# A sliding-window copy with DMA queues alone: twelve staged batches for eleven, half-window copies throughout, and the spilled halves last

## The chip, the cores and the metric

The kernel runs on one core of a Trainium2 chip. A core has engines that compute (TensorE, VectorE, ScalarE, GpSimd), SyncE, and 16 DMA engines that copy. Any of SyncE, ScalarE and GpSimd can issue a copy; each of the three has its own DMA queue, and all three queues are served by the same 16 DMA engines. The metric is the time of one execution on the device in microseconds (us).

## The reference

The input is 32 batches of 4096 rows of 256 floats. A window is 64 rows, and windows start every 32 rows, so each batch has 127 windows and every row but the first and the last 32 of a batch appears in two of them.

```
batch, length, dim = (32, 4096, 256)          # float32; window_size 64, stride 32
n_windows = (length - window_size) // stride + 1      # 127
result = np.zeros((batch, n_windows, window_size, dim), dtype=np.float32)
for i in range(n_windows):
    start = i * stride
    result[:, i] = x[:, start:start + window_size].copy()
```

Nothing is computed: 134 MB are read, and 266.3 MB are written. The unit of all that follows is a block of 32 rows, 32 KB. A batch is 128 blocks; window w of a batch is the blocks w and w + 1, its two halves.

## The kernel before, in words

Batches are copied in two ways.

A **direct** batch goes from DRAM to DRAM. `windows` (line 29) copies n consecutive windows, whole (64 KB each) or only half 0 or half 1 of each (32 KB each). Its argument `piece` is the largest run of one packet in bytes, 32 KB unless given. With 16 windows in a copy, each of the 16 DMA engines gets one window. `columns` (line 40) copies a few windows cut into 16 strips of 4 KB, so that each engine gets a strip of each window.

A **staged** batch goes through on-chip memory. `Staging` (line 70) has six buffers of 128 partitions x 32 KB. `load` puts block p of the batch into partition p (4 MB); `store` writes all 128 partitions out twice, once as half 0 and once as half 1 of the windows, in packets of 16 KB. A block is so read once and written twice. As there are 127 windows and 128 blocks, each of the two stores spills one half window over into the neighbouring batch: half 0 of block 127 lands in the first window of the next batch, and half 1 of block 0 in the last window of the batch before. So those two windows of the neighbours must be written after the stores have landed.

Three engines issue:

- ScalarE (`ring_s`, queue q10) runs `Staging.run`: in groups of six, first the loads of the group, then its stores. Staged are batches 1, 4, 7, ..., 31, eleven of them (the last with its blocks shifted by one, so that it takes along the last block of batch 30). A load waits for the stores that used its buffer before, a store waits for its load.
- SyncE (`ring_d`, queue q1) issues the direct batches in pieces of 16 windows, 147 of them (lines 175 to 190). A counter `share` chooses for each piece whether it goes out as one copy of whole windows or as two copies of halves: more halves while ScalarE's queue is expected to hold loads, fewer while it holds stores.
- GpSimd (`ring_r`, queue q0) starts when the last piece but one has landed (semaphore `near`, line 192) and copies the `edges` (15 windows of each direct batch beside a staged one, which include the windows that were spilled over), each after a wait for the stores of the staged neighbour. A copy of columns follows.

SyncE then waits for the stores of the last staged batch (line 202), copies two last windows as columns, and waits for all semaphores. A queue's packets are taken in order; between the queues an engine takes turns packet by packet. A copy ends on each engine with a completion packet of 4 bytes, which takes a turn as well.

The changed parts are `Staging.load` and `Staging.store` and everything from line 143 to the end of the kernel function.

Of the kernel before, what the change touches and what calls it, by code (L numbers as in the profile page):

```python
# [8 lines left out]
DIRECT, IN, OUT = 32768, 16384, 16384  # L9


class Copier:
# [36 lines left out]
    def load(self, q, t, b, c, rows):  # L49

        p, step, n, unit = rows
        return q.dma_start(
            out=t[p : p + (n - 1) * step + 1 : step, :],
            in_=self.xap(b * self.nb + c + p // unit, [[step // unit * self.blk, n], [1, self.blk]]),
            max_dma_last_dim=IN,
        )

    def store(self, q, t, b, c, rows, half):


        p, step, n, unit = rows
        w = b * self.nw + c + p // unit - half
        return q.dma_start(
            out=self.oap(2 * w + half, [[2 * step // unit * self.blk, n], [1, self.blk]]),
            in_=t[p : p + (n - 1) * step + 1 : step, :],
            max_dma_last_dim=OUT,
        )


class Staging:  # L70
# [14 lines left out]

    def load(self, q, g):
        i = g % len(self.tiles)
        b, c, n = self.items[g]
        if self.count[self.stored[i]]:
            q.wait_ge(self.stored[i], self.count[self.stored[i]])  # L90
        step = 128 // n
        parts = [(k, 4, 32, 1) for k in range(4)] if g == 0 else [(0, step, n, step)]
        for rows in parts:
            self.issue(self.c.load(q, self.tiles[i], b, c, rows), self.loaded[i])
        self.after_load[g] = self.count[self.loaded[i]]

    def store(self, q, g):
        i = g % len(self.tiles)
        b, c, n = self.items[g]
        q.wait_ge(self.loaded[i], self.after_load[g])  # L100
        step = 128 // n
        parts, end = [((0, step, n, step), 0), ((0, step, n, step), 1)], []
        if g == len(self.items) - 1:

            parts = [((0, 1, 128, 1), 1), ((0, 1, 32, 1), 0)]
            end = [(96, 1, 32, 1)] + [(32 + k, 4, 16, 1) for k in range(4)]
        for rows, half in parts:
            self.issue(self.c.store(q, self.tiles[i], b, c, rows, half), self.stored[i])
        for rows in end:
            self.issue(self.c.store(q, self.tiles[i], b, c, rows, 0), self.ended)  # L110
        self.after_store[g] = self.count[self.stored[i]]

    def wait_stored(self, q, g):
# [12 lines left out]
@with_exitstack  # L126
def kernel(
    ctx: ExitStack,
    tc: tile.TileContext,
    x: bass.AP,  # L130
    window_size: bass.AP,
    stride: bass.AP,
    out: bass.AP,
):
    nc = tc.nc
    W, S = int(window_size), int(stride)
    B, L, D = x.shape
    n_win = (L - W) // S + 1
    assert out.shape == (B, n_win, W, D)
    c = Copier(x, out, B, L, D, W, S, n_win)  # L140


    staged = [*range(1, B, 3)]
    items = [(b, -1 if b == B - 1 else 0, c.nb) for b in staged]
    place = {b: g for g, (b, _, n) in enumerate(items) if n == c.nb}
    direct = [b for b in range(B) if b not in staged]
    pool = ctx.enter_context(tc.tile_pool(name="xb", bufs=1))
    st = Staging(c, tc, pool, x.dtype, items, 6)
    ring_d, ring_s, ring_r = nc.sync, nc.scalar, nc.gpsimd
    done = tc.alloc_semaphore("done")  # L150
    near = tc.alloc_semaphore("near")
    rest = tc.alloc_semaphore("rest")
    total = {done: 0, near: 0, rest: 0}

    def count(dma, sem):
        dma.then_inc(sem, 16)
        total[sem] += 16

    sixteens = []
    for b in direct:
        w = 15 if b - 1 in staged else 0
        sixteens += [(b, w + 16 * j) for j in range((c.nw - w) // 16)]
    singles = [(B - 1, c.nw - 1, 1)]
    edges = [(b, 0 if b - 1 in staged else 112, 15) for b in direct[:-1]]
    last = B - 2
    edges.append((last, 112, 4))

    first_loads, loads, stores = 6 * 17, 5 * 17, 6 * 34  # L170
    turns = share = 0
    with tc.tile_critical():  # L172
        st.run(ring_s)

        for i, (b, w) in enumerate(sixteens):
            sem = near if i == len(sixteens) - 2 else done
            second = turns - first_loads - stores
            loading = turns < first_loads or 0 <= second < loads
            share += 120 if turns < 16 or -8 <= second < 16 else 90 if loading else 18
            if share >= 120:  # L180
                share -= 120
                turns += 4
                count(c.windows(ring_d, b, w, 16, 0), done)
                count(c.windows(ring_d, b, w, 16, 1), sem)
            else:
                turns += 3
                count(c.windows(ring_d, b, w, 16), sem)
            if i == len(sixteens) // 2:
                for b, w, half in singles:
                    count(c.windows(ring_d, b, w, 1, half, 2048), done)  # L190

        ring_r.wait_ge(near, 16)
        for b, w, n in edges:
            for k in (b - 1, b + 1):
                if k in place and b != last:
                    st.wait_stored(ring_r, place[k])
            count(c.windows(ring_r, b, w, n), rest)


        count(c.columns(ring_r, last, 116, 9), rest)  # L200
        ring_r.drain()  # L201
        st.wait_stored(ring_d, place[B - 1])
        count(c.columns(ring_d, last, 125, 2), done)
        total[st.ended] = st.count[st.ended]
        for sem, n in total.items():
            ring_d.wait_ge(sem, n)
# [35 lines left out]
```

## Time and profile before

| | |
|---|---|
| time, median of 3 runs | 753.98 us (753.93 to 756.95) |
| span of the profiled execution | 742.1 us |
| time around the span, by the median | 11.9 us |
| copied by the DMA engines | 313.26 MB, mean 422 GB/s |
| memory read, written | 220.95 MB, 267.09 MB |
| copies issued by SyncE | 92 of 1024 KB, 110 of 512 KB, 2 small |
| copies issued by ScalarE | 14 loads, 27 stores |
| copies issued by GpSimd | 22 |
| first GpSimd copy issued | 649.1 us |
| SyncE's last copy issued | 723.8 us |

The time of a run is a little longer than the span of the profiled execution, which goes from the first to the last instruction. The page's DMA line shows in 40 equal slices how busy the 16 DMA engines were, in tenths. The table of queues gives for each queue its packets, its MB, and the time that its packets took as a share of the 16 engines' time over the span; so the shares add up to the whole when the engines are full. The same view can be asked for any stretch of the span. The trace also holds a record of every single packet with its start, its duration, its queue and its size.

### The profile page before, as it was taken

Reading aid. Unit: us, or ns where it says so; the run is one execution under the profiler, and the core shown is the slowest. Engines: PE = TensorE matmul, PEld = TensorE weight load, DVE = VectorE, ACT = ScalarE, POOL = GpSimd, SP = SyncE. Lnnn points to the kernel's source line nnn. Section 1 sums busy time; section 2 is a strip of 40 time slices with the busy share of each in tenths; the row PEclk is TensorE's granted clock in tenths of the full one; section 3 lists DMA queues with packets and bytes.
Section 4 is the critical chain, followed back from the end, with each engine's and each line's share of the span. In section 5 each row is a group of like instructions: output and inputs, shape, how many; then the busy total and the mean of one; then the engine's idle time right before and its main releaser. Section 6 shows DMA issues by size and latency. Waiting matters only on the chain.

```text
span 742.1 us, 323 instructions
## 1 busy us (share of the span) xinstructions
POOL 12.7 (2%) x26
## 2 busy tenths in 40 slices
POOL 0000000000000000000000000000000000050100
DMA  8999999999999999999999999999999999999996
GB/s 361 424 430 427 435 431 428 423 435 425 428 427 426 428 428 420 429 435 427 427 427 412 433 435 431 427 436 432 434 424 429 430 424 426 428 435 432 421 420 253
DMA packets 18290, 313.26 MB, mean 422 GB/s; under 512 B 4336, under 2 KB 4336, under 8 KB 4528
## 3 DMA queue, kind: packets, MB, share of 16 engines
q1 hardware_dynamic: 8016, 154.32, 48.8%
q10 hardware_dynamic: 9104, 138.41, 44.0%
q0 software_dynamic: 1168, 20.51, 6.6%
q14 instruction: 2, 0.02, 0.0%
HBM read 220.95 MB, written 267.09 MB: 658 GB/s over the span
## 4 chain that ended last, share of the span: by engine, by line
another core or an unknown queue 92%; POOL 2%; issue 0%; POOLq 0%; SPq 0%
POOL out_dram L34 2%; POOLq L201 0%; POOLq L237 0%; SPq L172 0%; POOLq L114 0%
## 5 line engine op out<-in xcount | busy, mean ns | idle before, releaser
L34 POOL DMA_DIRECT2D out_dram<-in_x_dram x21 | 12.0, 575 | 685.4 <-DMA out_dram<-in_x_dram 648.7
L44 POOL DMA_DIRECT2D out_dram<-in_x_dram x1 | 0.6, 581 | 0.0
L223 POOL MEMSET const-float32-0.0<- 128x1 f32 x1 | 0.1, 98 | 0.2 <-issue 0.2
L223 POOL MEMSET const-bfloat16-1.0<- 128x1 bf16 x1 | 0.1, 101 | 0.0
L223 POOL MEMSET const-float32-1.0<- 128x1 f32 x1 | 0.1, 98 | 0.0
L223 POOL MEMSET const-uint8-127<- 128x1 uint8 x1 | 0.1, 98 | 0.0
## 6 DMA issues: line engine op xcount, KB each, us to landing
out_dram<-in_x_dram SPq DMA_DIRECT2D x92, 1024.0 KB, 99.8
out_dram<-xb ACTq DMA_DIRECT2D x21, 4096.0 KB, 138.5
out_dram<-in_x_dram SPq DMA_DIRECT2D x110, 512.0 KB, 90.2
xb<-in_x_dram ACTq DMA_DIRECT2D x10, 4096.0 KB, 130.5
out_dram<-in_x_dram POOLq DMA_DIRECT2D x20, 960.0 KB, 37.9
xb<-in_x_dram ACTq DMA_DIRECT2D x4, 1024.0 KB, 15.7
out_dram<-xb ACTq DMA_DIRECT2D x2, 1024.0 KB, 110.5
out_dram<-xb ACTq DMA_DIRECT2D x4, 512.0 KB, 94.4
```

What stands on the lines that cost most here:

```text
L34: return q.dma_start(out=self.oap((b * self.nw + w0) * 2 + h, [[2 * blk, n], row]), in_=self.xap(b * self.nb + w0 + h, [[blk, n], row]), m ...
L44: return q.dma_start(out=self.oap((b * self.nw + w0) * 2, [[part, 16], [2 * self.blk, n], row]), in_=self.xap(b * self.nb + w0, [[part, 16 ...
L223: nc = _bacc.Bacc("TRN2", target_bir_lowering=False, num_devices=1)
```

## The change

Staged are now twelve batches: 1, 4, 7, 10, 13, 16, 18, 20, 22, 25, 28 and 30. `store` splits some of its two stores into two copies of 64 partitions (even and odd ones), in an alternating pattern, and the last batch's into four.

SyncE's direct copies, 280 now, are all of halves of 16 windows. The counter `share` is gone. Twenty halves at the end of the list are held back, and two more, `spoilt` (which contain the half windows that the stores of batch 30 spill over), are put last of all. SyncE issues 258 halves and a copy of columns, waits for the semaphore `back`, issues the twenty, waits for the first two stores of batch 30, and issues the two.

GpSimd starts when the fourth half from the end of the 258 has landed. Its list of 22 edges is preceded by three whole windows and eight windows in halves; the edges beside batch 28 are moved to the end of the list. Every third edge goes in 16 KB pieces. The semaphore `back` is raised by the 18th of the 22 edges.

```diff
     def store(self, q, g):
         i = g % len(self.tiles)
-        b, c, n = self.items[g]
+        b = self.items[g]
         q.wait_ge(self.loaded[i], self.after_load[g])
-        step = 128 // n
-        parts, end = [((0, step, n, step), 0), ((0, step, n, step), 1)], []
         if g == len(self.items) - 1:
-
-            parts = [((0, 1, 128, 1), 1), ((0, 1, 32, 1), 0)]
-            end = [(96, 1, 32, 1)] + [(32 + k, 4, 16, 1) for k in range(4)]
...
+            parts = [(0, 2, 1), (1, 2, 0), (0, 2, 0), (1, 2, 1)]
+        else:
+            parts = [(k, n, half) for half in (0, 1) for n in (2 if (2 * g + half) % 4 < 2 else 1,) for k in range(n)]
+        for m, (k, n, half) in enumerate(parts):
+            sem = self.ended if g == len(self.items) - 1 and m > 1 else self.stored[i]
+            self.issue(self.c.store(q, self.tiles[i], b, 0, (k, n, 128 // n, 1), half), sem)
...
-    staged = [*range(1, B, 3)]
-    items = [(b, -1 if b == B - 1 else 0, c.nb) for b in staged]
+    staged = [1, 4, 7, 10, 13, 16, 18, 20, 22, 25, 28, B - 2]
...
-    sixteens = []
+    sixteens, edges = [], []
+    last, held = B - 1, 20
     for b in direct:
-        w = 15 if b - 1 in staged else 0
-        sixteens += [(b, w + 16 * j) for j in range((c.nw - w) // 16)]
-    singles = [(B - 1, c.nw - 1, 1)]
-    edges = [(b, 0 if b - 1 in staged else 112, 15) for b in direct[:-1]]
-    last = B - 2
-    edges.append((last, 112, 4))
-
-    first_loads, loads, stores = 6 * 17, 5 * 17, 6 * 34
-    turns = share = 0
+        first = 0 if b == last or b - 1 not in staged else 7 if b + 1 in staged[:-1] else 15
+        sixteens += [(b, first + 16 * j) for j in range(7)]
+        if b != last:
+            edges += [(b, w, n) for w, n in ((0, first), (first + 112, 15 - first)) if n]
+    odd = -sum(n for _, _, n in edges) % 16
+    late = [e for e in edges if staged[-2] in (e[0] - 1, e[0] + 1)]
+    edges = [e for e in edges if e not in late] + late
+    halves = [(b, w, half) for b, w in sixteens for half in (0, 1)]
+    spoilt = [(last - 2, c.nw - 16, 1), (last, 0, 0)]
+    halves = [h for h in halves if h not in spoilt]
+    middle, main = len(halves) // 2, len(halves) - held
+
+    def blocks(part, sem=done):
+        for b, w, half in part:
+            count(c.windows(ring_d, b, w, 16, half), sem)
+
     with tc.tile_critical():
         st.run(ring_s)

-        for i, (b, w) in enumerate(sixteens):
-            sem = near if i == len(sixteens) - 2 else done
...
-            share += 120 if turns < 16 or -8 <= second < 16 else 90 if loading else 18
-            if share >= 120:
-                share -= 120
-                turns += 4
-                count(c.windows(ring_d, b, w, 16, 0), done)
-                count(c.windows(ring_d, b, w, 16, 1), sem)
-            else:
-                turns += 3
-                count(c.windows(ring_d, b, w, 16), sem)
...
+        blocks(halves[:middle])
+        count(c.columns(ring_d, last, 120 + odd, 7 - odd), done)
+        blocks(halves[middle : main - 4])
+        blocks(halves[main - 4 : main - 3], near)
+        blocks(halves[main - 3 : main])

         ring_r.wait_ge(near, 16)
+        count(c.windows(ring_r, last, 112, odd), rest)
+        for half in (0, 1):
+            count(c.windows(ring_r, last, 112 + odd, 8, half, DIRECT // 2), rest)
+        for i, (b, w, n) in enumerate(edges):
             for k in (b - 1, b + 1):
-                if k in place and b != last:
+                if k in staged[:-1]:
                     st.wait_stored(ring_r, place[k])
-            count(c.windows(ring_r, b, w, n), rest)
-
-
-        count(c.columns(ring_r, last, 116, 9), rest)
+            count(c.windows(ring_r, b, w, n, piece=DIRECT if i % 3 != 0 else DIRECT // 2), back if i == len(edges) - len(late) - 3 else rest)
         ring_r.drain()
-        st.wait_stored(ring_d, place[B - 1])
-        count(c.columns(ring_d, last, 125, 2), done)
+
+        ring_d.wait_ge(back, 16)
+        blocks(halves[main:])
+        st.wait_stored(ring_d, place[B - 2])
+        blocks(spoilt)
```

More of the change, by code (lines that the diff above doesn't have):

```diff
@@ L87, in load @@
         i = g % len(self.tiles)
-        b, c, n = self.items[g]
+        b = self.items[g]
         if self.count[self.stored[i]]:
             q.wait_ge(self.stored[i], self.count[self.stored[i]])
-        step = 128 // n
-        parts = [(k, 4, 32, 1) for k in range(4)] if g == 0 else [(0, step, n, step)]
+        parts = [(k, 4, 32, 1) for k in range(4)] if g == 0 else [(0, 1, 128, 1)]
         for rows in parts:
-            self.issue(self.c.load(q, self.tiles[i], b, c, rows), self.loaded[i])
+            self.issue(self.c.load(q, self.tiles[i], b, 0, rows), self.loaded[i])
         self.after_load[g] = self.count[self.loaded[i]]
@@ L98, in store @@
         i = g % len(self.tiles)
-        b, c, n = self.items[g]
+        b = self.items[g]
         q.wait_ge(self.loaded[i], self.after_load[g])
-        step = 128 // n
-        parts, end = [((0, step, n, step), 0), ((0, step, n, step), 1)], []
         if g == len(self.items) - 1:
-            parts = [((0, 1, 128, 1), 1), ((0, 1, 32, 1), 0)]
-            end = [(96, 1, 32, 1)] + [(32 + k, 4, 16, 1) for k in range(4)]
[L107 to L110, printed above, removed]
+            parts = [(0, 2, 1), (1, 2, 0), (0, 2, 0), (1, 2, 1)]
[4 more added lines that the diff above has]
+            self.issue(self.c.store(q, self.tiles[i], b, 0, (k, n, 128 // n, 1), half), sem)
         self.after_store[g] = self.count[self.stored[i]]
@@ L140 @@
     c = Copier(x, out, B, L, D, W, S, n_win)
-    staged = [*range(1, B, 3)]
-    items = [(b, -1 if b == B - 1 else 0, c.nb) for b in staged]
-    place = {b: g for g, (b, _, n) in enumerate(items) if n == c.nb}
+    staged = [1, 4, 7, 10, 13, 16, 18, 20, 22, 25, 28, B - 2]
+    place = {b: g for g, b in enumerate(staged)}
     direct = [b for b in range(B) if b not in staged]
     pool = ctx.enter_context(tc.tile_pool(name="xb", bufs=1))
-    st = Staging(c, tc, pool, x.dtype, items, 6)
+    st = Staging(c, tc, pool, x.dtype, staged, 6)
     ring_d, ring_s, ring_r = nc.sync, nc.scalar, nc.gpsimd
@@ L152 @@
     rest = tc.alloc_semaphore("rest")
-    total = {done: 0, near: 0, rest: 0}
+    back = tc.alloc_semaphore("back")
+    total = {done: 0, near: 0, rest: 0, back: 0}
     def count(dma, sem):
@@ L172 @@
     with tc.tile_critical():
         st.run(ring_s)
-        for i, (b, w) in enumerate(sixteens):
-            sem = near if i == len(sixteens) - 2 else done
-            second = turns - first_loads - stores
-            loading = turns < first_loads or 0 <= second < loads
-            share += 120 if turns < 16 or -8 <= second < 16 else 90 if loading else 18
-            if share >= 120:
-                share -= 120
-                turns += 4
-                count(c.windows(ring_d, b, w, 16, 0), done)
-                count(c.windows(ring_d, b, w, 16, 1), sem)
-            else:
-                turns += 3
-                count(c.windows(ring_d, b, w, 16), sem)
-            if i == len(sixteens) // 2:
-                for b, w, half in singles:
-                    count(c.windows(ring_d, b, w, 1, half, 2048), done)
+        blocks(halves[:middle])
@@ L192 @@
+        count(c.columns(ring_d, last, 120 + odd, 7 - odd), done)
+        blocks(halves[middle : main - 4])
+        blocks(halves[main - 4 : main - 3], near)
+        blocks(halves[main - 3 : main])
         ring_r.wait_ge(near, 16)
-        for b, w, n in edges:
+        count(c.windows(ring_r, last, 112, odd), rest)
+        for half in (0, 1):
+            count(c.windows(ring_r, last, 112 + odd, 8, half, DIRECT // 2), rest)
+        for i, (b, w, n) in enumerate(edges):
             for k in (b - 1, b + 1):
-                if k in place and b != last:
+                if k in staged[:-1]:
```

## The prediction, made before the changed kernel ran

> **What bounds the kernel now.** Nothing is computed; the 16 DMA engines copy, fed by three queues: q1 (SyncE, direct copies), q10 (ScalarE, staged batches), q0 (GpSimd, edges). I read the page's DMA line and queue table first, then the DMA view of three stretches, then the DMA queue's waits.
>
> ```profile
> DMA  8999999999999999999999999999999999999996
> DMA packets 18290, 313.26 MB, mean 422 GB/s; under 512 B 4336, under 2 KB 4336, under 8 KB 4528
> ## 3 DMA queue, kind: packets, MB, share of 16 engines
> q1 hardware_dynamic: 8016, 154.32, 48.8%
> q10 hardware_dynamic: 9104, 138.41, 44.0%
> q0 software_dynamic: 1168, 20.51, 6.6%
> ...
> HBM read 220.95 MB, written 267.09 MB: 658 GB/s over the span
> ```
>
> The engines are full from the first slice to the last: the three shares sum to 99.4% of 742.1 us, 737.7 us of packet time on each engine. They move 313.26 MB: a direct byte passes once (266.3 MB are the output), a staged byte twice, once as load and once as store. The single packets of the trace run from 2.4 to 739.7 us. What remains to be asked is whether an engine is slowed by memory or is at its own pace. The stretch 430 to 520 us:
>
> ```profile
> DMA packets 2321, 38.82 MB, mean 431 GB/s; under 512 B 589, under 2 KB 589, under 8 KB 589
> ## 3 DMA queue, kind: packets, MB, share of 16 engines
> q1 hardware_dynamic: 1162, 20.88, 54.0%
> q10 hardware_dynamic: 1159, 17.94, 46.5%
> ```
>
> 46.5% of 16 x 90 us is 669.6 us for 17.94 MB, 37.3 us per MB, or 0.611 us for a staged packet of 16,384 B. q1's is 37.2 us per MB, its completion packets included. The trace's packet records say the same: 98% of the 16 KB packets here take 0.611 us and 97% of the 32 KB packets 1.213 us, with 0.009 us for a completion packet. And 150 to 390 us:
>
> ```profile
> DMA packets 5700, 102.67 MB, mean 428 GB/s; under 512 B 1216, under 2 KB 1216, under 8 KB 1232
> ## 3 DMA queue, kind: packets, MB, share of 16 engines
> q1 hardware_dynamic: 2852, 58.89, 57.7%
> q10 hardware_dynamic: 2848, 43.78, 42.9%
> ```
>
> The same sums give 37.6 us per MB on both queues, 1% more: some packets are stalled (31% of the 32 KB ones). q1 has more of the engines here, because its whole-window copies give two 32 KB packets to one completion packet, and the queues take turns packet by packet. Last, 736 to 740 us, where one engine still works and the others are done:
>
> ```profile
> DMA packets 25, 0.11 MB, mean 29 GB/s; under 512 B 6, under 2 KB 6, under 8 KB 22
> ```
>
> Memory is nearly idle here, and the 16 KB packets still take 0.611 us. So 0.611 and 1.213 us are the engine's own pace, and nothing that spares memory makes a packet shorter. Over the run, 313.26 MB x 37.3 / 16 = 730 us; the 737.7 us measured are about 8 us of stalls above it. That is all that a gentler pattern can give back, besides an end in which 15 engines finish between 734 and 737 us and one at 739.7 (one was already 3 us behind the others at 652 us, where q1's main stream ends).
>
> ```profile
> SPq L44 <- DMA out_dram<-xb: 169.3, 1, 169.3
> SPq L206 <- DMA out_dram<-in_x_dram: 15.8, 1, 15.8
> ```
>
> SyncE idles 169.3 us before its last copy and nothing suffers, since the other queues keep the engines full.
>
> **The change, part by part**, in packet time per engine.
>
> *A twelfth staged batch.* Its load is 4 MB: 16 packets of 16 KB on each engine. Its stores are 32 more. 11 x 48 = 528 packets become 576: +48 x 0.611 = +29.3 us.
>
> *SyncE's copies.* 110 half-window copies and 92 whole-window ones are 294 packets of 32 KB; 280 halves (258, 20 held back, 2 spilled) are 280: -14 x 1.213 = -17.0 us. The two spilled halves are written twice: each staged batch stores 128 rows twice where its output has 127 windows, and that is inside the counts of both versions.
>
> *GpSimd's copies.* Before: 304 whole windows, 38 packets of 32 KB an engine, and a columns copy of nine 4 KB packets at 0.159 us. After: 3 + 8 + 285 = 296 windows, 37 packets: -1.2 - 1.4 us. SyncE's columns copy grows from two to four such packets: +0.3 us. Eight of the edges and the two half copies go in 16 KB or half-window pieces: 2 x 0.611 for 1.213, under +0.1 us.
>
> *Completion packets.* 267 copies become 281 + 53 + 25 = 359: +92 x 0.009 = +0.8 us, of which some overlaps (a packet starts 3 to 4 ns before the one before it ends): +0.5.
>
> Sum: +29.3 - 17.0 - 1.2 - 1.4 + 0.3 + 0.1 + 0.5 = **+10.6 us**. This lies wholly on the path that sets the end, as every engine is full throughout.
>
> *Issue.* 77 more copies on SyncE cost it 0.56 us each (its shortest issue), 43 us of a queue that finishes issuing at 554 us against 649 us for its last landing. Hidden by the roughly 90 us of packets queued ahead; without them they would cost up to 43 us. ScalarE's 12 more copies at 0.4 us go the same way.
>
> The Trainium skill, "DMA: Bandwidth & Descriptors", Anatomy of one DMA, speaks against halves: about 2.0 us fixed per DMA (measured there from GpSimd) plus bytes over 436 GB/s. By it, 92 more DMAs in series would be an estimated +184 us. The rows of 0.009 us with the engines full say that overlapping copies pay no such thing; the sum goes by the rows.
>
> *Stalls: halves only.* A 32 KB packet now alternates with a completion packet, and between them go two 16 KB packets: q1's share falls from 0.58 to near 0.52. Stretches that already look so: 20 to 125 us (53.0%, 429 GB/s) and 430 to 520 us (54.0%, 431). Bounds: -8 us (all as in 430 to 520) and +1 (halves bring nothing, one more percent of the added 10.6 and some collisions). The first packets (0.9 us of stall in 2 to 20 us), a bout at 400 to 420 (0.6 us) and the last 30 us (1.4 us) are in mixed or half-window stretches, so I leave them, and take **-3 us** off the stores' stretches, some half of what these have.
>
> *SyncE holds back and waits.* With turns taken packet by packet, 258 halves against staged packets end near 610 us, when about 103 staged packets (63 us), 37 of GpSimd's (45 us) and 22 held or spilled ones (27 us) remain. GpSimd's edges wait for the stores of batches 22, 25 and 28 in turn, and SyncE for the 18th edge; behind SyncE's wait are 20 halves, the wait for batch 30's first two stores, the two spilled halves and the end. While they wait, q10 has packets: no idle engine. Cost 0. At the end, the last two stores are 16 packets (9.8 us alone), which cover the wake-up, issue and first packet of the spilled halves (about 1.5 us from issue to packet for SyncE's last copy, then 2.4 us). Uncovered, they would cost 2.4 us and a landing (3.6 us at least for line 34) on top: +6. Lower bound: -4, if the slow engine's lag of 3 to 4 us went. I take **-0.6**: it lags with the stalls.
>
> Sum: +10.6 - 3 - 0.6 = +7.0. The span becomes 749.1 us; the profiled execution has 11.9 us around its span by the median of 753.98 us, so 761.0 us.
>
> **Rivals.** *Memory is the bound.* Then time goes with memory traffic: reads fall to 166.5 (direct) + 50.3 (loads) = 216.8 MB, writes stay at 267.1, 483.9 for 488.05 MB: -0.85%, -6.3 us, 747.7 us. For it: the 1% stalls come where q1's share is high. Against: 77% of all 32 KB packets are at 1.213 us, and a lone engine is no faster. The skill's same page, Where 436 GB/s comes from, says that memory binds HBM to SBUF transfers, at about 358 GB/s a core; the 431 GB/s above disagree. By that rule the sum would be this rival's.
>
> *The stalls go altogether.* +10.6 - 8 = +2.6, less 2 of the lag: 754.6 us, no change. It decides if the long store stretches run at 431 GB/s as 430 to 520 does. Against it: 20 to 125 us, rich in halves too, is at 429, and the last 30 us were stalled with q1 empty.
>
> *An uncovered end.* Should the waits of GpSimd on stores and of SyncE on GpSimd chain, with q10 drained first, the held halves run late and alone: +7.0 + 3 to 6, so 764 to 767 us.
>
> **How the numbers follow.** 0.5% of the time, 3.8 us, is about what a measurement here can tell: 750.2 to 757.8. Forecast (757.8 to 764) 0.70, uncovered end 0.13, both slower; stalls gone 0.12; memory-bound 0.04, faster; 0.01 of the rest to faster. So slower 0.83, same 0.12, faster 0.05. The range, 755 to 766, reaches into the stall-free case and the uncovered end; the forecast's own is 757.8 to 764.
>
> **What would show it.** About 317.5 MB with shares that sum to some 99%, q10 near 151 MB and q1 near 147, and a mean still of 422 to 426 GB/s; MB per share at 37.3 to 37.6; q1's share near 0.52 up to some 600 us; the first GpSimd copy about 40 us earlier than 649 us. Wrong if the mean rises over 430 GB/s (stalls gone), if packets fall under 0.611 us, or if slices near the end show under 9 (uncovered).

## The result, and the profile after

The changed kernel takes 755.99 us (median of 20 runs, 755.0 to 758.62), the kernel before 753.89 us (20 runs, 751.1 to 756.95): a ratio of 1.0035, with an interval of 1.0024 to 1.0046. It is slower by 2.1 us, which lies inside the 0.5% (3.8 us) that the prediction called no change, and not the 7.0 us that it gave. The time itself lies at the low end of the stated 755 to 766 us. In a later group of runs, all on one chip, the ratio was 1.0060 (1.0047 to 1.0072): 754.97 against 750.78 us, 4.2 us. The two intervals don't overlap: the kernel before was 3 us faster in the later group, the changed one 1 us.

The page of the changed kernel, its DMA lines and its queues:

```profile
DMA  8999999999999999999999999999999999999997
GB/s 359 416 427 430 431 431 432 427 434 432 431 431 431 431 431 431 431 431 431 411 428 429 429 431 431 428 428 431 431 431 434 431 424 412 430 431 415 396 418 257
DMA packets 20562, 317.50 MB, mean 421 GB/s; under 512 B 5982, under 2 KB 5982, under 8 KB 6046
## 3 DMA queue, kind: packets, MB, share of 16 engines
q10 hardware_dynamic: 10064, 151.00, 47.2%
q1 hardware_dynamic: 9040, 147.08, 46.1%
q0 software_dynamic: 1456, 19.40, 6.2%
```

The bytes and their division among the queues are what was forecast (317.5, 151 and 147 MB); the mean of 421 GB/s is just under the 422 to 426. Two things are to be seen in the second line: from the fifth to the nineteenth slice it stands between 427 and 434, mostly at 431, and near the end it drops to 412, 415 and 396. The main stream and the end, each in its DMA view:

```profile
DMA packets 12783, 200.02 MB, mean 430 GB/s; under 512 B 3683, under 2 KB 3683, under 8 KB 3747
...
q1 hardware_dynamic: 6392, 103.69, 52.1%
q10 hardware_dynamic: 6390, 96.32, 48.5%
```

This is 130 to 595 us. q1 has 52.1% of 16 x 465 us for 103.69 MB, 37.4 us per MB, against 37.3 for unstalled packets; only 1.5 us of stalls an engine lie between 130 and 597 us. (A stall here and below is what a packet record has above its own size's pace, 1.213, 0.611 or 0.159 us, and 0.309 us for 8 KB, summed and divided by 16.) The last 12 us, 740 to 752:

```profile
DMA packets 194, 2.88 MB, mean 240 GB/s; under 512 B 106, under 2 KB 106, under 8 KB 106
...
q1 hardware_dynamic: 192, 2.88, 66.3%
q10 hardware_dynamic: 2, 0.00, 0.0%
```

Staged packets are gone, and SyncE's last halves run alone: 66.3% of 16 x 12 us for 2.88 MB are 44 us per MB. SyncE's waits say how they came to be last:

```profile
SPq L34 <- DMA out_dram<-in_x_dram: 163.2, 1, 163.2
...
SPq L34 <- DMA out_dram<-xb: 12.1, 1, 12.1
```

SyncE had issued its 258 halves by 532 us and waited 163.2 us for the 18th edge, which GpSimd had issued at 619.1 us; the twenty held halves were issued from 694.7 us on, the two spilled ones at 719.4 us. The last staged packet ended at 740.7 us, the last half at 751.7 us.

One more number: this execution took 755.18 us with a span of 753.4, so 1.8 us lie around a span, not the 11.9 us that the prediction used.

### The profile page after: what moved, and what is told of

Its sections match the earlier page's. It is cut to its first block, busy times and chain, and to the rows that moved or that the text cites. A ratio compares the mean times of both kernels' runs of the same rounds, so it can differ in the third digit from the quotient of the medians.

```text
span 753.4 us, 420 instructions
## 1 busy us (share of the span) xinstructions
POOL 14.5 (2%) x29
## 4 chain that ended last, share of the span: by engine, by line
another core or an unknown queue 90%; POOL 2%; issue 0%; POOLq 0%; SPq 0%
POOL out_dram L34 2%; POOLq L194 0%; POOLq L233 0%; SPq L176 0%
## 5 line engine op out<-in xcount | busy, mean ns | idle before, releaser
L34 POOL DMA_DIRECT2D out_dram<-in_x_dram x25 | 14.3, 575 | 677.7 <-DMA out_dram<-in_x_dram 607.3
## 6 DMA issues: line engine op xcount, KB each, us to landing
xb<-in_x_dram ACTq DMA_DIRECT2D x4, 1024.0 KB, 16.1
```

The lines of the kernel that those rows point to most:

```text
L34: return q.dma_start(out=self.oap((b * self.nw + w0) * 2 + h, [[2 * blk, n], row]), in_=self.xap(b * self.nb + w0 + h, [[blk, n], row]), m ...
```

## The experiments

**The kernel before, profiled again.** No edit.

> The kernel before, profiled once more, since its profiled span (742.1 us) and its median time (753.9 us) lie 11.9 us apart, while the changed kernel's profiled span (753.4 us) and its own time (755.18 us) lie 1.8 us apart. Theory A (the first profiled execution was a short one, and ordinary ones have about 10 us more of stalled packets): span about 751 to 753 us, packet time of the three queues about 745 to 748 us an engine against 737.7. Theory B (12 us lie around the span of this kernel): span 742 us again with a time of 754 us.

> The kernel before, a third profile, on the same chip as a2. Theory A (ordinary executions stall 14 to 18 us, and the first profiled one with 8 us was an exception): span 747 to 752 us, packets' time 744 to 748 us an engine. If the first profile is as common: span near 742 us.

Measured: spans of 748.1 and 748.3 us with times of 749.83 and 750.12 us. The page's queues and the stretch 130 to 640 us of the second of them:

```profile
DMA packets 18290, 313.26 MB, mean 419 GB/s; under 512 B 4336, under 2 KB 4336, under 8 KB 4528
## 3 DMA queue, kind: packets, MB, share of 16 engines
q1 hardware_dynamic: 8016, 154.32, 48.9%
q10 hardware_dynamic: 9104, 138.41, 44.1%
q0 software_dynamic: 1168, 20.51, 6.6%
```

```profile
DMA packets 12255, 216.03 MB, mean 424 GB/s; under 512 B 2767, under 2 KB 2767, under 8 KB 2783
...
q1 hardware_dynamic: 6127, 121.68, 56.6%
q10 hardware_dynamic: 6126, 94.34, 43.9%
```

Theory A holds, though the first of the two spans is 3 us below the 751 to 753 us that it gave. Both queues pay 38.0 us per MB here (56.6% of 16 x 510 us for 121.68 MB), for 37.3 at full pace. An engine's packet time is 745.3 and 745.1 us, its stalls 15.5 and 15.3 us, twice the 7.6 us of the execution that the prediction was worked out from. In that one the same stretch reads:

```profile
DMA packets 12393, 218.46 MB, mean 428 GB/s; under 512 B 2794, under 2 KB 2794, under 8 KB 2810
...
q1 hardware_dynamic: 6191, 122.89, 56.5%
q10 hardware_dynamic: 6200, 95.55, 44.0%
```

The shares are the same, the rate is higher. The span of that first execution is about 10 us below what 753.9 us of time leave for one; 6 of these 10 us are seen in the two later profiles. The times of these two lie below the medians of the kernel's groups of runs (750.7 to 753.9 us) as well. If all that an execution takes longer is stalls, the median one holds, by an estimate from these times and the 1.8 us, 16 to 19 us of them.

**The changed kernel once more**, in the group of the second of these. No edit.

> The changed kernel once more, beside the others of this group on one chip. Theory S: 3 to 8 us of stalls fewer than the kernel before in the same group (1 to 2 us from 130 us to GpSimd's first packet, for 10 or so), 10 to 11 us more of packet work, time 1 to 5 us above the kernel before.

Measured: ratio 1.0060, span 754.6 us. An engine's packet time is 751.6 us, 10.9 of them stalls. Against the kernel before on the same chip (745.1 and 15.3):

| us per engine | before | after | difference |
|---|---|---|---|
| packets without stalls | 729.8 | 740.7 | +10.9 |
| stalls, first 20 us | 0.8 | 1.0 | +0.2 |
| stalls, from 20 us to 15 us before GpSimd's first packet | 12.0 | 3.0 | -9.0 |
| stalls, from there to the end | 2.4 | 6.9 | +4.4 |
| packet time | 745.1 | 751.6 | +6.5 |

The spans differ by 6.3 us. So the added work is as large as forecast, the main stream gives back most of it, and the end takes half of that away. The first profile of the changed kernel against that of b1 gives the same picture (-9.6 and +3.9 us). Of the 6.9 us at the end, 2.0 fall before SyncE's held halves are issued at 697 us, 1.5 from there to 728 us, mostly with three queues at work, and 3.4 after that.

The 6.3 us are more than the 4.2 us of the medians: the execution of the changed kernel that was profiled took 756.38 us, 1.4 above its median, and that of the kernel before 750.12 us, 0.7 below. The table shows where stalls went; the size of the change is the medians'.

**Whole windows in the changed kernel.** `blocks` merges two halves of the same piece that stand together:

```diff
-        for b, w, half in part:
-            count(c.windows(ring_d, b, w, 16, half), sem)
+        part = list(part)
+        while part:
+            b, w, half = part.pop(0)
+            if half == 0 and part and part[0] == (b, w, 1):
+                part.pop(0)
+                half = None
+            count(c.windows(ring_d, b, w, 16, half, DIRECT), sem)
```

> The changed kernel with SyncE's direct copies as whole windows of 64 KB wherever both halves of a piece stand together (126 of its 129 pairs in the main stream), the rest as it is. Theory S (the stalls follow q1's share of the engines' turns): q1's share rises from 0.52 to about 0.58 up to some 540 us, its 32 KB packets there average 1.23 to 1.25 us for 1.213, and 8 to 12 us of stalls an engine come in that stretch; time 3 to 8 us above the changed kernel. Theory W (how a window is split has no influence; the stalls of the kernel before come from its batches and edges): no stall there, time within 2 us of the changed kernel.

Measured: ratio 1.0314 (1.0290 to 1.0339), 774.38 us, 19.4 us above the changed kernel's 754.97 on the same chip. The stretch 130 to 545 us:

```profile
DMA packets 9418, 172.13 MB, mean 415 GB/s; under 512 B 1937, under 2 KB 1937, under 8 KB 2001
...
q1 hardware_dynamic: 4708, 100.96, 58.7%
q10 hardware_dynamic: 4709, 71.16, 41.8%
```

q1's share is 58.7%, its price 38.6 us per MB, and q10's 39.0. The stalls are 16.5 us in this stretch alone (4.0%) and 28.6 us in all. Theory S holds in kind, and its 3 to 8 us were too few.

**Whole windows in 16 KB packets**: the same edit with `DIRECT // 2`. This tells whether whole windows stall or the share does.

> As before with whole windows, but in packets of 16 KB: each whole window is four packets and a completion packet, so q1's share falls to about 0.45. Theory S: no stalls (under 0.2%) in the main stream although the windows are whole; q1 and GpSimd's queue are left for the end, where direct packets run alone for some 70 us and stall by about 20%, so that the time is 8 to 16 us above the changed kernel. Theory H (two packets of one window in a row stall by themselves, whatever the share): stalls of 1 to 2% in the main stream.

Measured: 771.04 us in one run. The main stream, 130 to 650 us, and the stretch 690 to 760 us:

```profile
DMA packets 16012, 224.07 MB, mean 431 GB/s; under 512 B 2288, under 2 KB 2288, under 8 KB 2352
...
q10 hardware_dynamic: 8012, 120.26, 54.0%
q1 hardware_dynamic: 7999, 103.80, 46.7%
```

```profile
DMA packets 1723, 22.71 MB, mean 324 GB/s; under 512 B 592, under 2 KB 592, under 8 KB 592
## 3 DMA queue, kind: packets, MB, share of 16 engines
q0 software_dynamic: 996, 13.27, 57.9%
q1 hardware_dynamic: 727, 9.44, 40.8%
```

Whole windows at a share of 46.7% run at 431 GB/s with 0.1% of stalls: theory H falls. With no staged packets left, the direct ones pay 48 to 49 us per MB on both queues and 23% of the time is stalls. The total, 16.1 us above the changed kernel's 754.97, is at the upper end of the 8 to 16 us that were expected.

**Halves at a high share.**

```diff
-DIRECT, IN, OUT = 32768, 16384, 16384
+DIRECT, IN, OUT = 32768, 8192, 8192
```

> The changed kernel, halves only, with the staged packets cut to 8 KB (loads and stores). q1 then passes 32 KB per two turns against 16 KB of q10, a share near 0.66. Theory S: stalls of 2 to 5% in the main stream, which ends near 490 us, and a time 15 to 30 us above the changed kernel with the stalls summing to 15 to 30 us. Theory H: halves are free of stalls at any share, so only the added packets count, under 5 us.

Measured: 801.63 us in one run. 130 to 500 us:

```profile
DMA packets 12115, 145.69 MB, mean 394 GB/s; under 512 B 3276, under 2 KB 3276, under 8 KB 3340
...
q1 hardware_dynamic: 6060, 98.32, 68.2%
q10 hardware_dynamic: 6054, 47.37, 32.5%
```

Halves alone do not protect: at a share of 68.2% q1 pays 41.1 us per MB, its 32 KB packets average 1.337 us, and 8.4% of the stretch are stalls: theory H falls again. Theory S was too low as well: it gave 15 to 30 us of stalls and a time as much above the changed kernel, and 53.5 us of stalls and 46.7 us came. Staged packets of 8 KB then ran nearly alone from 558 to 658 us.

**Halves only in the kernel before**, with its eleven staged batches.

```diff
-            share += 120 if turns < 16 or -8 <= second < 16 else 90 if loading else 18
+            share += 120
```

> The kernel before (eleven staged batches) with all of SyncE's copies as halves, its one part of the change alone. Work of the packets as in the kernel before (+0.5 us for 92 more completion packets). Theory S: the main stream up to some 640 us has q1's share at 0.52 and almost no stall (about 1 us for the 10 to 12 us of the kernel before), but some 50 to 70 direct packets an engine are left when q10 is done, which pass at 1.45 to 1.48 us, 12 to 18 us of stalls; time within -4 and +4 us of the kernel before. Theory W: the same stalls as the kernel before through the main stream, time +10 us or more, since the end comes on top.

Measured: ratio 1.0130 (1.0108 to 1.0152), 760.55 us. 20 to 670 us:

```profile
DMA packets 17663, 279.20 MB, mean 430 GB/s; under 512 B 5005, under 2 KB 5005, under 8 KB 5021
...
q1 hardware_dynamic: 8827, 144.13, 51.8%
q10 hardware_dynamic: 8834, 135.06, 48.8%
```

The stalls of the main stream are gone as in the changed kernel (2.8 us from 130 to 676 us, for 10 us from 130 to 650 us in the kernel before), so halves, by the share that they give q1, account for nearly all of that gain. But q10 is done at 675.5 us, and q1's rest and GpSimd's edges run alone for 80 us at 20 to 23% of stalls, 15.9 us. The miss is in the size: the time is 6 us above the upper end that theory S gave. Eleven batches leave too little to run beside the direct copies at that share. The changed kernel has a twelfth, and is 5.6 us faster than this one; it differs in its edges and its order too, so the twelfth batch's own part in these 5.6 us isn't shown.

**No wait on `back`.** The line `ring_d.wait_ge(back, 16)` is taken out.

> The changed kernel without SyncE's wait for the semaphore back: the 20 held halves follow the 258 at once. Theory C (the held halves run alone at the end, about 15 packets at 1.48 us instead of 1.21, some 5 us in all): the last 20 us no longer hold a stretch of q1 alone; but three queues together put two direct packets against one staged one for about 60 us, which would stall by up to 9%, 5 us. Net -3 to +1 us against the changed kernel. Theory D (the end costs nothing, the time is the bulk of the work): within 1 us of the changed kernel, with the same stalled share.

Measured: ratio 1.0053 (1.0037 to 1.0070). The end no longer holds q1 alone, but between 627 and 677 us the three queues run together at a direct share of 0.69 (34.7% of the engines for q1, 34.1% for q0) and 9.6% of the time is stalls, 4.8 us. From 732 us on there is almost none. The hold moves stalls from the middle of the end to its last 20 us; it neither costs nor gains much.

**GpSimd's edges in 32 KB pieces**, in two groups of runs.

```diff
-piece=DIRECT if i % 3 != 0 else DIRECT // 2
+piece=DIRECT
```

> The changed kernel with all of GpSimd's edges in 32 KB pieces. Taking turns with staged packets, its edges pass in about 8 rounds fewer (28 to 30 packets of direct copies an engine for 37), so back comes some 10 us earlier and more staged packets are left beside the held halves. Theory C: 2 to 4 us less than the changed kernel, and fewer packets at 1.48 us in the last 20 us. Theory D: no change (under 1 us).

> The changed kernel with GpSimd's edges all in 32 KB pieces, in one group with the changed kernel. Theory C (held halves alone at the end stall): 1 to 3 us less than the changed kernel, the saving in the last 50 us. Theory D: within 0.5 us.

Measured: ratios 1.0026 (1.0014 to 1.0039) and 1.0032 (1.0021 to 1.0042); in the second group the changed kernel stood at 1.0060, so that this version is 1.8 us below it (753.19 against 754.97 us). Its stalls are 7.2 us for 10.9, and 1.4 for 3.4 us from 728 us on. The last 24 us, first of the changed kernel and then of this version:

```profile
DMA packets 488, 7.57 MB, mean 315 GB/s; under 512 B 229, under 2 KB 229, under 8 KB 229
...
q1 hardware_dynamic: 415, 6.65, 77.6%
q10 hardware_dynamic: 73, 0.92, 10.2%
```

```profile
DMA packets 452, 6.80 MB, mean 283 GB/s; under 512 B 179, under 2 KB 179, under 8 KB 179
...
q1 hardware_dynamic: 300, 4.65, 50.3%
q10 hardware_dynamic: 152, 2.15, 21.7%
```

More staged packets stand beside the held halves: theory C. SyncE's wait got 7 us shorter (157.2 us for 163.9). Only half of the stalls saved comes out as time: the span is 4.9 us longer than an engine's packet time here and 3.0 us in the changed kernel; from 744 us on the engines of this version are less than half busy.

**Fourteen halves held, released by the 21st edge.**

```diff
-    last, held = B - 1, 20
+    last, held = B - 1, 14
...
-back if i == len(edges) - len(late) - 3 else rest
+back if i == len(edges) - 2 else rest
```

> The changed kernel with 14 halves held back for 20, and the semaphore back raised by the 21st edge for the 18th, so that SyncE comes in when GpSimd is nearly done and never are three queues at work for long. Theory S: q1's share of the last 120 us spreads out, the stall of the three-queue stretch (1.4 us in 25 us) goes and some halves still end alone; 0 to 3 us less than the changed kernel. Theory D: within 0.5 us.

Measured: ratio 1.0059 (1.0046 to 1.0071), the changed kernel's. The three-queue stall goes, as expected, but the release comes at 720.9 us, and with q10 done at 731.8 us the halves end alone again: 3.5 us of stalls from 716 to 741 us. It only moves them, as the run without a hold did. No version tried is below the kernel before.

**What the stretches say together.** Direct bytes are read from and written to memory, staged ones cross it once per packet. The profile's own count of memory agrees: for the kernel before, 2 x 174.83 MB of direct and 138.41 MB of staged packets are 488.07 MB, and it counts 220.95 read and 267.09 written, 488.04. From the lines shown, per stretch:

| stretch | q1's share | us per MB of q1 | GB/s copied | memory GB/s (2 x direct + staged) |
|---|---|---|---|---|
| whole windows in 16 KB, 130 to 650 | 46.7% | 37.4 | 431 | 630 |
| eleven batches, halves, 20 to 670 | 51.8% | 37.4 | 430 | 651 |
| after, 130 to 595 | 52.1% | 37.4 | 430 | 653 |
| before, first profile, 130 to 640 | 56.5% | 37.5 | 428 | 669 |
| before, later profile, 130 to 640 | 56.6% | 38.0 | 424 | 662 |
| whole windows in 32 KB, 130 to 545 | 58.7% | 38.6 | 415 | 658 |
| halves beside 8 KB packets, 130 to 500 | 68.2% | 41.1 | 394 | 659 |
| direct copies alone, 690 to 760 | all (with q0) | 49 | 324 | 649 |

Up to a share of 52% the engines hold 430 to 431 GB/s and memory goes up with the share. Above it memory stands at 649 to 669 GB/s, and the copied rate falls. So there are two walls, one of the engines and one of memory, and they meet near a direct share of 0.53 (660 / 431 = 1.53).

It is read and write together that count, not one of them. The run with whole windows of 32 KB shows it, first while its staged packets are loads alone (40 to 100 us), then while they are stores alone (160 to 300 us; q10 takes its packets in order, and the first 25.2 MB of it are the loads of six batches):

```profile
DMA packets 1330, 24.99 MB, mean 416 GB/s; under 512 B 252, under 2 KB 252, under 8 KB 252
...
q1 hardware_dynamic: 666, 14.65, 57.9%
q10 hardware_dynamic: 664, 10.34, 42.8%
```

```profile
DMA packets 3179, 58.17 MB, mean 415 GB/s; under 512 B 684, under 2 KB 684, under 8 KB 686
...
q1 hardware_dynamic: 1590, 34.65, 60.0%
q10 hardware_dynamic: 1588, 23.51, 40.6%
```

Memory reads 416 and writes 244 GB/s in the first, and reads 248 and writes 415 in the second; the sums are 661 and 663, and both have 3.9% of stalls.

Not every stall fits. The changed kernel stalls below the wall too: at 20 to 40 us (3.5% at 629 GB/s), between stores and loads at 360 to 380 us (3.8% at 624 GB/s), and while GpSimd's edges and staged packets are alone at 620 to 640 us (4.0% at 625 GB/s). What makes them is open.

The Trainium skill, "HBM Reference", Specifications (TRN2), gives about 716 GB/s for the memory that two cores share. No stretch of the table came above 669. The skill's "DMA: Bandwidth & Descriptors", Where 436 GB/s comes from, gives a ceiling of 435 GB/s for the 16 ports through which the engines reach on-chip memory. The 431 GB/s measured lie 1% below it; whether direct copies, which don't end in on-chip memory, are held by the same ports no run here shows.

## Why the prediction was wrong, point by point

*The packets of the change, +10.6 us: right.* Packet time without stalls rose by 10.9 us (740.7 for 729.8). The twelfth batch, the 14 packets fewer of SyncE and the completion packets are priced as the trace of before had them; 92 more copies cost nothing else that can be seen.

*"The profiled execution has 11.9 us around its span": wrong.* 1.8 us lie around a span. The other 10 us were missing from the execution that was profiled, and the step added them to both kernels as if they were fixed. As far as profiles show it (6 of the 10 us), what was missing is stalls, and stalls are what the change acts on. The gap between span and median stood in the table, and its size was the warning. So the span was forecast 4.3 us too short (749.1 for 753.4 us) and the time 5.0 us too long (761.0 for 755.99 us).

*"About 8 us of stalls above it. That is all that a gentler pattern can give back": wrong, for the same reason, and the step that failed first.* Later executions had 15.3 and 15.5 us, 12 of them in the main stream of each.

*"-3 us off the stores' stretches, some half of what these have": mis-sized.* The direction and the mechanism were right, and q1's share fell to the forecast 0.52. But at 0.52 nearly all of the main stream's stalls go, -9.0 us. The stores' stretches (125 to 400 and 520 to 652 us) had 3.7 us in the execution that was read, so that 3 us are four fifths of them and not half; in the later one they have 8.9 us, and the changed kernel has 0.8 left there. The term took most of too small a stock.

*"SyncE holds back and waits ... Cost 0": wrong.* The end measured +4.4 us of stalls from shortly before GpSimd's first packet on. (The -0.6 us for the lagging engine was of no weight: the spans differ by 6.3 us where the mean packet times differ by 6.5.) No engine idled for long, as foreseen, but an engine that is full of direct packets alone is not at its pace (44 us per MB from 740 to 752 us). The step asked only if queues run empty, and its sign, slices under 9, can't show this: only the last slice was. It also set no time for the eighteenth edge: the held halves were issued from 694.7 us on, since the edges of 15, 8 and 7 windows took 39 to 66 us to land (medians by size) in turns with q10, and with 16 KB pieces GpSimd's queue moves less per turn. The piece size was priced at under 0.1 us as work; as turns it costs 1.8 us, as the run with 32 KB pieces shows. Two readings were off without weight: SyncE's last copy took 4.0 us from its issue at 723.8 us to its first packet at 727.8, not about 1.5, and the 1.4 us of stalls stand in the last 42 us and not 30.

*The sum +7.0: near the profiles by luck.* The two profiles compared differ by 6.3 us, since the stalls that went and were not counted (6.0 us) and those that came and were not counted (4.4 us) largely cancel in them. The medians, 2.1 and 4.2 us, are those of executions in which the kernel before stalls more.

*The rivals.* The order "stalls go altogether: 754.6 us, no change" came nearest, but it was not what happened: the main stream's stalls went and the end brought others. "An uncovered end" did happen in its mechanism: q10 drained first, the held halves ran late and alone, and the +4.4 us are within its 3 to 6; its time came out too high since it stood on the same +7.0. "Memory is the bound" was set aside because most packets are at their pace and a lone engine is no faster. Both are true and neither settles it: close to the wall only some packets wait (31% of the 32 KB ones in the stretch shown), and their mean is what counts. In the two later profiles of the kernel before, the memory wall did set the pace of the main stream, by 2%. Taking stalls away there, the change ran into the engines' wall, which its twelfth batch had moved up. By estimates from the rates in the table, 313.26 MB at 431 GB/s are 727 us and 488.05 MB of memory traffic at 662 GB/s are 737 us for the kernel before; 317.5 MB are 737 us and 483.9 MB of traffic 731 us after. So the change trades one wall for another of the same height, and the end decides.

*GpSimd's first copy* was issued at 607.7 us, 41 us earlier than before, as forecast.

Open: why the first profiled execution of before had half the stalls at the same shares. With 1.8 us around it, it would have taken 743.9 us; the 20 times of its kernel start at 751.1 us, and two later profiles did not repeat it. Open too is why the kernel before took 753.9 us by the median of the first runs and 750.8 us in the last group. Nor was it tried to hold the edges so that neither three queues nor one alone are ever at work; the versions tried only moved that stall.

## What to carry to other kernels

Set the span of the profiled execution against the times before any sum is made on it: where the gap is larger than another profile of the same kind of kernel shows, the execution profiled was not a usual one, and its stalls must not be taken as the stock. A copy kernel has two walls, bytes through the DMA engines and bytes through memory, and both should be worked out for the kernel as a whole and for each stretch, its end too; a mix is good where both are just reached. With queues that take turns packet by packet, the sizes of packets and the completion packets between them set that mix; the runs that changed the order of issue at the end only moved the stalls.

## What the runs showed of the hardware that was not expected

Memory traffic, read and written together, stood at 649 to 669 GB/s whenever the mix asked for more, from a direct share of 57% up to direct copies alone, while the engines went from 428 to 324 GB/s. The step is steep: 0.3 to 0.4% of the time is stalls at a share of 52%, 2% at 56.6% (0.8% in the first execution), 4% at 58.7%, 8.4% at 68.2% and 20 to 23% with direct copies alone. A 4-byte completion packet takes 0.009 us of an engine and yet moves the mix by several per cent, since it takes a turn: q1 and q10 have 6392 and 6390 packets in the stretch of the changed kernel, and 4708 and 4709 in that with whole windows, completion packets counted. With one per 32 KB packet q1 has 52% of the engines, with one per two 58.7%.
